# A hierarchical mixture-of-experts block: float32 rows kept once, a later residual, two more weight slots

## The chip, the cores and the metric

The kernel runs on one core of a Trainium2 chip. The metric is the device time of one launch in microseconds (us). The engines that matter are TensorE (PE in the rows, its weight loads PEld), VectorE (DVE), ScalarE (ACT), GpSimd (POOL) and SyncE (SP), whose queue issues the large loads from HBM. All data is float32 in HBM; all weights are read once.

## The reference

One layer over 256 latent tokens of width 1024. A mixing half (retention over tokens and a 256-token context, a convolution branch, gates, an output projection) gives `mix`; then

```python
h_lat = _layernorm(ALPHA * h_lat + gt_m * mix, p['ln1_g'], p['ln1_b'])
moe = _hier_moe(_modulate(h_lat, sh_f, sc_f), p)
h_lat = _layernorm(ALPHA * h_lat + gt_f * moe, p['ln2_g'], p['ln2_b'])
```

`_hier_moe` picks for each token the best of four groups and the two best of its eight experts, and adds up, weighted, what the 32 experts give:

```python
for e in range(N_EXPERTS):
    h = jax.nn.silu(t @ p['w_exp_gate'][e]) * (t @ p['w_exp_up'][e])
    y = y + combine[:, e:e + 1] * (h @ p['w_exp_down'][e])
```

An expert has a gate and an up matrix of 1024 x 512 and a down matrix of 512 x 1024, 2 MiB each.

## The kernel before

The mixing half fills PE until about 511 us. Its result plus ALPHA times the input is `xr`, two tiles of 128 tokens by 1024. Then comes the **head of the experts**, once: the statistics of the first layer norm and the router's scores; two calls of `rank` on DVE (groups, then experts in the group), which give the mask `M`; three small matmuls on PE (`ppos`) that turn the mask into each token's place among an expert's tokens; and `gather(0)`.

The normalized rows are kept without the layer norm's gain and bias (these and the modulation are in the columns `fsc` and `fsh`). They are kept as a pair: `xr` is normalized in place (one tile on ACT, one on POOL), `xns[0]` is its value rounded to fp32r, a shorter float format, and `xns[1]` is what the rounding left out, also in fp32r; POOL forms half of that (`xn_low(G, ...)`), DVE the rest in two pieces. The sum of both products gives a float32 row to enough places. After gather 0 is set up, DVE overwrites `xr` with ALPHA times the layer norm's full result, the residual `yacc`; for this PE has spread the gain and bias `ln1` over all partitions (`lnb`, eight K=1 matmuls of a high and low part).

`gather(c)` serves experts 4c to 4c+3. DVE writes a one-hot matrix (`ohr`, later `ohq`) of 256 places; for each of eight slices k of the width, PE multiplies the rows with it (line 1351: two token tiles times two parts, four matmuls of 128 x 128 by 256), and ACT or DVE moves the result out with scale and bias into `xe[c]`. It is a generator that yields after every two k, so four pieces of it are spread over a pair of experts.

The experts run in 16 pairs, e0 = 0, 2, ..., 30, in `expert_pair`: gate and up of the one (`hidden`, line 1365: 64 places as stationary columns, in two halves side by side), of the other, transposes, and the down products (line 1465). What the down products give is put back to tokens one pair later by `scatter` (line 1406), into four PSUM banks that collect over all pairs; `flush` adds them to `yacc` in the last pair. Every second pair (e0 = 2, 6, ..., 26) carries the gather of the next four experts. After pair e0 = 28 a branch on a count of tokens leads to `overflow()`, which this data doesn't need. The second layer norm's gain and bias (`ln2`) are loaded after pair e0 = 16 and spread by PE after pair e0 = 20 (line 1635), each of four banks copied out by ACT.

The **weights** come in tiles of 1 MiB, twelve to a pair (eight of gate and up, four of down), in the order of use (`plan`). `load_to(n)` puts loads up to the nth on SP's queue, in order; the tags of the list `slots` say which SBUF buffer each takes. A load waits until the last reader of its buffer's former tenant is done, and all behind it on the queue wait too. `first` has 19 entries; after that each turn has 16, from the 100th tile on 15, as other tiles need buffers. Tiles 0 to 18 are asked for before the experts begin (`NL`), the rest at the start and the end of every pair.

Of the kernel before, what the change touches and what calls it, by code (L numbers as in the profile page):

```python
# [8 lines left out]
F32 = mybir.dt.float32  # L9
# [10 lines left out]
P = 128  # L20
# [14 lines left out]
NL = 9, 5, 0, 6, 6, 5, 7, 8, 19, 6  # L35
NCYC = 100
# [3 lines left out]
LN2 = 16, 20  # L40
# [5 lines left out]
def tile_block(ctx, tc, a, out):  # L46
# [30 lines left out]
    def gload(dst, src):  # L77
        nc.gpsimd.dma_start(dst, src)
# [871 lines left out]
    def rows_load2(_):  # L950
        for q in range(2):
            ln1[q] = row1(f"ln1_{q}")
            G.memset(ln1[q], 0.0)
            for i, nm in enumerate(("ln1_g", "ln1_b")):
                gload(ln1[q][64 * i:64 * i + 33:32], a[nm].rearrange("o (c q f) -> q (o c) f", c=2, q=2)[q])
# [20 lines left out]
    ln1 = {}  # L976
# [294 lines left out]
    xn_low(V, 1, 1)  # L1271
# [14 lines left out]
    lnb = {}  # L1286
    for cb in range(2):
        for i in range(2):
            lnb[i, cb] = bank("y", f"lnb{i}{cb}")
            p0 = 64 * i + 32 * cb  # L1290
            for q in range(2):
                T.matmul(lnb[i, cb], oner[p0:p0 + 1], lns[q][p0:p0 + 1], start=(q == 0), stop=(q == 1))
# [3 lines left out]
    ppos = bank("gu", "ppos", (P, 2, 32))  # L1296
# [40 lines left out]
    def gather(c):  # L1337
        ohr = ohrs[c] = ohq[:, c % 2] if c else sb.tile([P, 2, 4, CAP], F32R, tag="rope", name="ohr", bufs=1)
# [3 lines left out]
        xe[c] = big("X8" if c == 1 else "U8", [P, 8, 4 * CAP], f"xe{c}")  # L1342
# [3 lines left out]
        for k2 in (2, 3, 0, 1):  # L1346
            ps = bank("mi", f"ga{c}_{k2}", (P, 2, 4 * CAP))
            for kk in range(2):
                k = 2 * k2 + kk
                for i, (t, s) in enumerate(((0, 0), (0, 1), (1, 0), (1, 1))):  # L1350
                    T.matmul(ps[:, kk], xns[s][:, t, k // 4, k % 4], ohr[:, t], start=(i == 0), stop=(i == 3))  # L1351
            for kk in range(2):
                k = 2 * k2 + kk
                if kk and c:
# [62 lines left out]
    def expert_pair(e0, side):  # L1417
# [5 lines left out]
        else:  # L1423
            hs = [hidden(e0)]
            if last:
                for cb in range(2):
                    scatter(e0 - 2, cb)
                flush()
# [97 lines left out]
    def overflow():  # L1526
# [12 lines left out]
        for k in range(8):  # L1539
            for s in range(2):  # L1540
                pt = bank("mi", f"oxt{k}_{s}", (P, 2, P))
                for t in range(2):
                    T.transpose(pt[:, t], xns[s][:, t, k // 4, k % 4].bitcast(F32), ident)
                if s == 0:
                    V.tensor_copy(xoT[:, k], pt)
                else:
                    V.tensor_add(xoT[:, k], xoT[:, k], pt)
            V.tensor_scalar(xoT[:, k], xoT[:, k], fsc[:, k:k + 1], fsh[:, k:k + 1], op0=ALU.mult, op1=ALU.add)
# [40 lines left out]
    xn_low(V, 1, 0)  # L1589

    yacc = xr
    for cb in range(2):
        cs = slice(512 * cb, 512 * cb + 512)
        for i, op in enumerate((ALU.mult, ALU.add)):
            for t in range(2):
                if i:
                    V.scalar_tensor_tensor(yacc[:, t, cs], lnb[1, cb], ALPHA, yacc[:, t, cs], op0=ALU.mult, op1=op)
                else:
                    V.scalar_tensor_tensor(yacc[:, t, cs], xr[:, t, cs], ALPHA, lnb[0, cb], op0=ALU.mult, op1=op)
# [3 lines left out]
    def rest():  # L1603
# [3 lines left out]
        V.tensor_copy(ohq[:, 0], ohrs[0].bitcast(F32))  # L1607
# [6 lines left out]
    ln2 = None  # L1614
    for e0 in range(0, NE, 2):
# [11 lines left out]
        if e0 == LN2[0]:  # L1627
            ln2 = big("Y8", [P, 2, D], "ln2")
            gload(ln2[0:1, 0], a["ln2_g"])
            gload(ln2[0:1, 1], a["ln2_b"])  # L1630
        if e0 == LN2[1]:
# [64 lines left out]
```

## Time and profile before

| | us |
|---|---|
| three runs | 996.44, 996.86, 998.81 |
| median | 996.86 |
| the profiled execution, its own time | 1000.41 |
| its span in the trace | 998.6 |
| PE busy in the span | 942.7 (94%) |
| DVE busy | 506.3 (51%) |
| ACT busy | 310.2 (31%) |
| POOL busy | 104.4 (10%) |
| mean granted TensorE clock | 0.977 |

PE is the busy engine of the span as a whole. The span has three stretches with different limits: the mixing half up to 511 us, the head of the experts up to 529 us, where little runs beside the chain through DVE, and the experts, in whose second half the DMA engines move 420 GB/s without a break. Which of two limits holds in the experts is read from the waits at single weight tiles and from the lengths of pairs, since a share of busy time averages over all of this.

### The profile page before, as it was taken

Reading aid. Unit: us, or ns where it says so; the run is one execution under the profiler, and the core shown is the slowest. Engines: PE = TensorE matmul, PEld = TensorE weight load, DVE = VectorE, ACT = ScalarE, POOL = GpSimd, SP = SyncE. Lnnn points to the kernel's source line nnn. Section 1 sums busy time; section 2 is a strip of 40 time slices with the busy share of each in tenths; the row PEclk is TensorE's granted clock in tenths of the full one; section 3 lists DMA queues with packets and bytes.
Section 4 is the critical chain, followed back from the end, with each engine's and each line's share of the span. In section 5 each row is a group of like instructions: output and inputs, shape, how many; then the busy total and the mean of one; then the engine's idle time right before and its main releaser. Section 6 shows DMA issues by size and latency. Waiting matters only on the chain. (4 is left out here: it accounts for less than half of the span.)

```text
span 998.6 us, 15317 instructions
## 1 busy us (share of the span) xinstructions
PE 942.7 (94%) x6354; PEld 691.5 (69%) x6354; DVE 506.3 (51%) x976; ACT 310.2 (31%) x458; POOL 104.4 (10%) x122
## 2 busy tenths in 40 slices
PE   3999999999999999989989999999999989999884
PEld 2799879779879869889976655656565554655452
DVE  1377988897886996785884111222221111222135
ACT  3357735443543444375443111111110101111010
POOL 1002120210210020721520000000000000000001
PEclk9699999999999999999999999999999998999998
DMA  8795634544374347759986899999999999999991
GB/s 269 231 362 202 220 107 129 214 143 160 115 253 142 136 139 239 268 185 289 348 331 272 346 419 419 421 420 420 420 419 420 421 419 421 421 420 420 421 366 44
DMA packets 92424, 294.81 MB, mean 295 GB/s; under 512 B 6921, under 2 KB 37825, under 8 KB 68288
## 3 DMA queue, kind: packets, MB, share of 16 engines
q1 hardware_dynamic: 91360, 293.31, 76.4%
q0 software_dynamic: 992, 0.49, 0.4%
q8 instruction: 51, 0.84, 0.4%
q14 instruction: 21, 0.17, 0.1%
HBM read 292.71 MB, written 1.06 MB: 294 GB/s over the span
## 5 line engine op out<-in xcount | busy, mean ns | idle before, releaser
L1465 PE MATMUL dn<-wdown,hT 128*64 128x512 f32 (+1 forms) x528 | 120.7, 584 | 6.3 <-DMA wdown<-in_w_exp_down_dram 6.0
L1365 PE MATMUL gu<-wgate,xe 128*64 128x256 f32 x1024 | 122.5, 391 | 2.2 <-DVEq L1625 2.2
L1365 PE MATMUL gu<-wup,xe 128*64 128x256 f32 x1024 | 118.3, 380 | 4.2 <-DMA wup<-in_w_exp_up_dram 4.1
L1371 DVE TENSOR_TENSOR h<-h,gu 128x256 f32<-128x256 f32 x32 | 13.5, 421 | 198.2 <-ACT h L1370 198.2
L404 DVE SCALAR_TENSOR_TENSOR slab<-zp,taps,slab 128x256 f32<-128x256 f32 x232 | 107.1, 515 | 0.0
L1365 PEld LDWEIGHTS gu<-wgate,xe 128*64 128x64 f32 x1024 | 74.5, 141 | 45.8 <-issue 10.3
L1365 PEld LDWEIGHTS gu<-wup,xe 128*64 128x64 f32 x1024 | 74.1, 137 | 42.8 <-DMA wup<-in_w_exp_up_dram 8.2
L1465 PEld LDWEIGHTS dn<-wdown,hT 128*64 128x64 f32 x528 | 37.6, 136 | 76.6 <-issue 59.9
L1370 ACT ACTIVATE h<-gu 128x256 f32<-128x256 f32 x32 | 12.3, 385 | 210.9 <-PE gu L1365 210.8
L1480 DVE SCALAR_TENSOR_TENSOR dl<-dn,ws,ohq 128x512 fp32r<-128x512 f32 x30 | 22.5, 751 | 104.3 <-ACT ohq L1479 104.3
L1479 ACT ACTIVATE ohq<-dn,ws 128x512 fp32r<-128x512 f32 x30 | 20.6, 688 | 125.4 <-PE dn L1465 122.7
L98 PE MATMUL ya<-rT,qro 128*128 128x256 f32 x128 | 36.7, 286 | 2.6 <-DVE rT L750 2.6
L97 PE MATMUL glu<-ulh,qz 128*128 128x256 f32 x128 | 37.5, 293 | 0.0
L99 PE MATMUL ya<-rT,qro 128*128 128x256 f32 x128 | 36.6, 286 | 0.8 <-DVE qro L164 0.8
L97 PE MATMUL ya<-rT,qro 128*128 128x256 f32 x128 | 36.9, 288 | 0.0
L99 PE MATMUL gt<-ulh,qg 128*128 128x256 f32 x128 | 35.8, 280 | 1.1 <-DVE qg L164 1.1
L98 PE MATMUL glu<-ull,qz 128*128 128x256 f32 x128 | 36.8, 287 | 0.0
L99 PE MATMUL glu<-ulh,qz 128*128 128x256 f32 x128 | 36.7, 287 | 0.0
L97 PE MATMUL gt<-ulh,qg 128*128 128x256 f32 x128 | 36.6, 286 | 0.0
L1358 ACT ACTIVATE xe<-ga,cf 128x256 f32<-128x256 f32 x36 | 19.8, 564 | 52.5 <-PE ga L1351 52.5
L98 PE MATMUL gt<-ull,qg 128*128 128x256 f32 x128 | 35.8, 279 | 0.0
L1351 PE MATMUL ga<-ohq,xnh 128*128 128x256 f32 x112 | 30.4, 306 | 0.0
(477 smaller groups left out, 2159.1 us busy)
## 6 DMA issues: line engine op xcount, KB each, us to landing
wgate<-in_w_exp_gate_dram SPq DMA_DIRECT2D x64, 1024.0 KB, 19.8
wup<-in_w_exp_up_dram SPq DMA_DIRECT2D x64, 1024.0 KB
wdown<-in_w_exp_down_dram SPq DMA_DIRECT2D x60, 1024.0 KB, 19.8
wa<-in_w_ada_dram SPq DMA_DIRECT2D x24, 1024.0 KB, 9.4
wz<-in_w_in_dram SPq DMA_DIRECT2D x16, 512.0 KB, 7.5
wro<-in_w_ret_out_dram SPq DMA_DIRECT2D x8, 1024.0 KB
wg<-in_w_in_dram SPq DMA_DIRECT2D x8, 1024.0 KB, 9.9
wk<-in_w_in_dram SPq DMA_DIRECT2D x4, 1024.0 KB, 12.3
```

The costliest lines, as they stand in the source:

```text
L97: T.matmul(ps, st[0], mv[0], start=start, stop=False)
L98: T.matmul(ps, st[0], mv[1], start=False, stop=False)
L99: T.matmul(ps, st[1], mv[0], start=False, stop=stop)
L404: V.scalar_tensor_tensor(dst, zp[:, ct, j:j + NT], taps[:, ct, j:j + 1], ac[ct], op0=ALU.mult, op1=ALU.add)
L1351: T.matmul(ps[:, kk], xns[s][:, t, k // 4, k % 4], ohr[:, t], start=(i == 0), stop=(i == 3))
L1358: S.activation(xe[c][:, k], ps[:, kk], AF.Identity, scale=fsc[:, k:k + 1], bias=fsh[:, k:k + 1])
L1365: T.matmul(ps[64 * hf:64 * hf + 64, j], xe[c][:, k, CAP * i:CAP * i + CAP], w[:, k % 4, NT * hf:NT * hf + NT], start=start, stop=stop)
L1370: S.activation(h, ps[:, 0], AF.Silu)
L1371: V.tensor_mul(h, h, ps[:, 1])
L1465: T.matmul(ps[64 * x:64 * x + 64], hT[x][:, ch % 2, 64 * (ch // 2):64 * (ch // 2) + 64], w, start=(ch == 0), stop=(ch == 3))
L1479: S.activation(dh, ps, AF.Copy, scale=ws)
L1480: V.scalar_tensor_tensor(dl, ps, ws, dh.bitcast(F32), op0=ALU.mult, op1=ALU.subtract)
```

## The change

Three things are changed.

- **The rows are kept once.** `xn` is one float32 tile pair, written by four ACT operations straight from the unnormalized `xr`. The split, POOL's and DVE's subtractions, and the split and the eight broadcasts of `ln1` are gone. `gather` multiplies `xn` and the one-hot as full float32: two matmuls for each k instead of four. The two matmuls that put zeros into the first experts' banks are written ahead of `ppos`; in gather 0 the odd slices are now moved out by DVE, as in the other gathers.
- **The residual is formed in the middle of the experts.** `ln1` is loaded after pair e0 = 14 into a tile `lnv`; after pair e0 = 18 PE spreads it with four K=1 matmuls (`l1r`), and DVE forms the new tile `yacc` from these and `xn` with eight operations. `ln2` is loaded into the same `lnv` after pair e0 = 20 and spread after pair e0 = 24.
- **Two more slots.** `first` has 21 entries, the turns after it 19, from the 96th tile on 17, the last 24 tiles 12. One weight tile (the ninth) is asked for two steps earlier in the output projection. `flush` and the scatter of pair e0 = 28 are written between gate and up of expert 30, no longer between the experts 30 and 31.

The core of the diff:

```diff
-NL = 9, 5, 0, 6, 6, 5, 7, 8, 19, 6
-NCYC = 100
+NL = 9, 5, 0, 6, 6, 5, 7, 9, 21, 6
+NCYC = 96
-LN2 = 16, 20
+LNS = 14, 20, 18, 24
...
-    body = ["X8"] + ["W8"] * 3 + ["Q8", "W8"] + ["Q8"] * 2 + ["X8"] * 2
-    first = ["S8", "X8"] + ["Y8"] * 4 + ["zp", "U8"] + body + ["Y8"]
-    cyc = ["S8", "X8"] + ["Y8"] * 3 + body[1:] + ["Y8"]
-    slots = first + ["S8", "X8"] + ["Y8"] * 4 + ["U8"] + body[1:] + ["Y8"]
+    body = ["W8"] * 3 + ["Q8", "W8"] + ["Q8"] * 2 + ["X8"] * 2
+    first = ["S8", "X8"] + ["Y8"] * 4 + ["zp"] + ["U8"] * 2 + ["X8"] + body + ["Y8"] * 2
+    full = ["S8", "X8"] + ["Y8"] * 4 + ["U8"] * 2 + body + ["Y8"] * 2
+    cyc = ["S8", "X8"] + ["Y8"] * 3 + ["U8"] * 2 + body + ["Y8"]
+    slots = first + full
     while len(slots) < NCYC:
-        slots += ["S8", "X8"] + ["Y8"] * 4 + body[1:] + ["Y8"]
+        slots += full
...
-            if cb == 1 and kq == 0:
+            if cb == 0 and kq == 2:
                 step(lambda _: load_to(NL[7]))
...
-    xns = [big("U8", [P, 2, D], f"xn{s}", F32R).rearrange("p t (r k q) -> p t r k q", r=2, k=4) for s in "hl"]
-
-    def xn_low(E, t, r):
-        E.tensor_sub(xns[1][:, t, r], xrk[:, t, r], xns[0][:, t, r].bitcast(F32))
+    xn = big("U8", [P, 2, D], "xn").rearrange("p t (r k q) -> p t r k q", r=2, k=4)
...
-    S.activation(xr[:, 0], xr[:, 0], AF.Identity, scale=rs1[:, 0:1], bias=nb1[:, 0:1])
-    G.tensor_scalar(xr[:, 1], xr[:, 1], rs1[:, 1:2], nb1[:, 1:2], op0=ALU.mult, op1=ALU.add)
-    for t in range(2):
-        S.activation(xns[0][:, t], xrk[:, t], AF.Copy)
-    xn_low(G, 0, slice(0, 2))
+    for r in (1, 0):
+        for t in range(2):
+            S.activation(xn[:, t, r], xrk[:, t, r], AF.Identity, scale=rs1[:, t:t + 1], bias=nb1[:, t:t + 1])
...
-                for i, (t, s) in enumerate(((0, 0), (0, 1), (1, 0), (1, 1))):
-                    T.matmul(ps[:, kk], xns[s][:, t, k // 4, k % 4], ohr[:, t], start=(i == 0), stop=(i == 3))
+                for t in range(2):
+                    T.matmul(ps[:, kk], xn[:, t, k // 4, k % 4], ohr[:, t].bitcast(F32), start=(t == 0), stop=(t == 1))
...
+        if e0 == LNS[2]:
+
+            yacc = big("Y8", [P, 2, D], "yacc")
+            for cb in range(2):
+                cs = slice(512 * cb, 512 * cb + 512)
+                yk = yacc[:, :, cs].rearrange("p t (q k) -> p t k q", k=4)
+                for i in range(2):
+                    ps = bank("mi", f"l1r{cb}{i}")
+                    T.matmul(ps, onef[0:1], lnv[0:1, i, cs], start=True, stop=True)
+                    pk = ps.rearrange("p (q k) -> p k q", k=4)
+                    for t in range(2):
+                        if i == 0:
+                            V.scalar_tensor_tensor(yk[:, t], pk, ALPHA, xn[:, t, cb], op0=ALU.mult, op1=ALU.mult)
+                        else:
+                            V.scalar_tensor_tensor(yacc[:, t, cs], ps, ALPHA, yacc[:, t, cs],
+                                                   op0=ALU.mult, op1=ALU.add)
```

How the instructions stand at two places, in the order of each engine's queue (a number behind a tile's name only tells buffers apart). PE in the head, from the broadcasts to the first gather, before:

```order
L1292 MATMUL lnb_4896<-lns_4786,oner 128x512
L1283 MATMUL clkq_4899<-oner,ident 128x128 x6
L1297 LDWEIGHTS tri
L1297 MATMUL ppos<-M,tri 128x32
L1298 LDWEIGHTS oneh
L1298 MATMUL ppos<-M,oneh 128x32
L1299 LDWEIGHTS tri
L1299 MATMUL ppos<-M,tri 128x32
L1283 MATMUL clkq_4910<-oner,ident 128x128 x5
L1351 MATMUL ga_2_4935<-ohr,xnh 128x256
L1351 MATMUL ga_2_4935<-ohr,xnl 128x256
```

and after:

```order
L1272 MATMUL gu_4874<-oner,zero 128x512
L1272 MATMUL gu_4875<-oner,zero 128x512
L1267 MATMUL clkq_4878<-oner,ident 128x128 x6
L1277 LDWEIGHTS tri
L1277 MATMUL ppos<-M,tri 128x32
L1278 LDWEIGHTS oneh
L1278 MATMUL ppos<-M,oneh 128x32
L1279 LDWEIGHTS tri
L1279 MATMUL ppos<-M,tri 128x32
L1267 MATMUL clkq_4889<-oner,ident 128x128 x5
L1331 MATMUL ga_2_4905<-ohr,xn 128x256 x4
L1331 MATMUL ga_3_4912<-ohr,xn 128x256 x4
```

Eight broadcasts are gone, the two zero matmuls (`gu`) stand ahead of `ppos`, and a bank of the gather (`ga`, two k) has four matmuls from one `xn` instead of eight from `xnh` and `xnl`.

DVE in the same place, from the second rank's first product to the end of the head, before:

```order
L1253 TENSOR_TENSOR rkec<-rkec,before 128x128
L1254 TENSOR_TENSOR rkec<-rkec 128x128
L1255 TENSOR_REDUCE rke<-rkec 128x16
L1269 TENSOR_SCALAR m_4858<-rke 128x16
L1263 TENSOR_TENSOR M<-m_4858,og 128x64
L1215 TENSOR_TENSOR xnl<-xr,xnh 128x512
L1340 TENSOR_TENSOR ohr<-ppos,slot 128x256 x2
L1344 COPY pos<-ppos 128x64
L1215 TENSOR_TENSOR xnl<-xr,xnh 128x512
L1599 SCALAR_TENSOR_TENSOR xr<-xr,lnb_4887 128x512 x2
L1597 SCALAR_TENSOR_TENSOR xr<-lnb_4890,xr 128x512 x2
```

and after:

```order
L1238 TENSOR_TENSOR rkec<-rkec,before 128x128
L1239 TENSOR_TENSOR rkec<-rkec 128x128
L1240 TENSOR_REDUCE rke<-rkec 128x16
L1254 TENSOR_SCALAR m_4846<-rke 128x16
L1248 TENSOR_TENSOR M<-m_4846,og 128x64
L1320 TENSOR_TENSOR ohr<-ppos,slot 128x256 x2
L1324 COPY pos<-ppos 128x64
L1335 TENSOR_SCALAR xe_4903<-ga_2_4905,cf 128x256
L1335 TENSOR_SCALAR xe_4903<-ga_3_4912,cf 128x256
```

The two subtractions (`xnl`) and the residual (`xr`, `lnb`) have left this place; the gather's own copies follow the one-hot `ohr`.

PE between pair e0 = 18 and the next, after (before, the gate follows the last matmul of the gather):

```order
L1443 MATMUL dn_1_6541<-wdown_1_6386,hT_6510 64x512
L1331 MATMUL ga_1_6553<-ohq,xn 128x256 x4
L1605 MATMUL l1r_6577<-lnv,oner 128x512
L1605 MATMUL l1r_6581<-lnv,oner 128x512
L1605 MATMUL l1r_6585<-lnv,oner 128x512
L1605 MATMUL l1r_6589<-lnv,oner 128x512
L1345 MATMUL gu_6601<-wgate_0_6388,xe_6408 64x256 x8
```

The four broadcasts `l1r` stand between the last piece of the gather and the gate of expert 20.

## Rows read from the trace of the kernel before

**Rows 1.** Windows of the core: length, busy us by engine, clock, DMA share, GB/s.
```profile
600.50:653.00 52.50, 52.50 (x389) 31.92 (x388) 10.71 (x24) 6.55 (x12) 0.00 (x0) 1.00 1.01 420
758.20:949.20 191.00, 179.83 (x1205) 101.31 (x1204) 33.62 (x76) 22.73 (x41) 1.08 (x2) 0.98 1.01 420
```

**Rows 2.** Timeline of PE, pairs e0 = 16 and 20: start, us, instruction, idle before.
```profile
758.20 1.08 PE L1465 MATMUL dn<-wdown,hT 128*64 128x512 f32 x4
...
823.12 5.36 PE L1465 MATMUL dn<-wdown,hT 128*64 128x512 f32 x22 [1.41 <-DMA wdown<-in_w_exp_down_dram]
828.41 1.12 PE L1635 MATMUL l2r<-ln,oner 1*128 1x512 f32 x2
...
833.79 6.29 PE L1365 MATMUL gu<-wgate,xe 128*64 128x256 f32 x32
839.92 3.62 PE L1365 MATMUL gu<-wup,xe 128*64 128x256 f32 x32
```

**Rows 3.** Timeline of PE, end of pair e0 = 28, gate of expert 30.
```profile
943.79 5.36 PE L1465 MATMUL dn<-wdown,hT 128*64 128x512 f32 x22 [1.42 <-DMA wdown<-in_w_exp_down_dram]
951.33 5.36 PE L1365 MATMUL gu<-wgate,xe 128*64 128x256 f32 x32 [2.17 <-DVEq L1625]
```

**Rows 4.** PE's waits from 540 us on: total, times, longest.
```profile
PE dn L1465 <- DMA wdown<-in_w_exp_down_dram: 6.0, 6, 1.4
PE gu L1365 <- DMA wup<-in_w_exp_up_dram: 4.1, 7, 1.2
```

**Rows 5.** Windows as in group 1: gather 0, behind the broadcasts, expert 30's gate.
```profile
832.30:839.10 6.80, 6.80 (x28) 3.05 (x29) 0.00 (x0) 1.13 (x2) 0.00 (x0) 0.50 1.01 417
951.80:955.20 3.40, 3.40 (x19) 2.41 (x17) 0.00 (x0) 0.00 (x0) 0.00 (x0) 0.50 1.02 419
524.65:528.20 3.55, 3.55 (x18) 3.47 (x17) 3.55 (x7) 1.02 (x2) 0.00 (x0) 0.50 0.01 2
```

**Rows 6.** Timeline of SP's queue, the last issue ahead of the experts.
```profile
511.64 19.75 SPq L75 DMA_DIRECT2D wup<-in_w_exp_up_dram  x2
```

**Rows 7.** Timeline of PE, one piece of gather 1 and the gate behind it.
```profile
561.93 0.38 PE L1351 MATMUL ga<-ohq,xnh 128*128 128x256 f32 x1
...
562.26 0.28 PE L1351 MATMUL ga<-ohq,xnh 128*128 128x256 f32 x1
...
562.83 0.28 PE L1351 MATMUL ga<-ohq,xnl 128*128 128x256 f32 x1
563.04 3.24 PE L1365 MATMUL gu<-wgate,xe 128*64 128x256 f32 x28
```

**Rows 8.** Timeline of PE, a retention product in full float32.
```profile
169.03 7.07 PE L686 MATMUL o<-v,dp 128*128 128x256 f32 x32
```

**Rows 9.** Timeline of DVE in the head of the experts.
```profile
518.02 0.28 DVE L1252 TENSOR_TENSOR rkec<-ig 128x128 f32<-128x128 f32 x1
518.22 2.95 DVE L1253 TENSOR_TENSOR rkec<-rkec,before 128x128 f32<-128x128 f32 x1
...
522.30 1.07 DVE L1215 TENSOR_TENSOR xnl<-xr,xnh 128x512 fp32r<-128x512 f32 x1
...
526.24 1.30 DVE L1597 SCALAR_TENSOR_TENSOR xr<-lnb,xr 128x512 f32<-128x512 f32 x2
```

**Rows 10.** Timeline of POOL in the head.
```profile
518.09 2.93 POOL L1215 TENSOR_TENSOR xnl<-xr,xnh 128x1024 fp32r<-128x1024 f32 x1 [2.06 <-ACT xnh L1241]
```

**Rows 11.** Timeline of PE in the head: ppos, gather 0, zeros, first gate.
```profile
522.44 0.18 PE L1297 MATMUL ppos<-M,tri 128*128 128x32 bf16 x1 [4.03 <-DVE M L1263]
...
524.65 0.56 PE L1351 MATMUL ga<-ohr,xnh 128*128 128x256 f32 x1
...
528.34 0.80 PE L1385 MATMUL gu<-xnh,zero 1*128 1x512 f32 x2
529.07 1.30 PE L1365 MATMUL gu<-wgate,xe 128*64 128x256 f32 x10
```

**Rows 12.** Timeline of ACT in the head.
```profile
515.96 3.99 ACT L1241 ACTIVATE xnh<-xr 128x1024 fp32r<-128x1024 f32 x2
```

More of the change, by code (lines that the diff above doesn't have):

```diff
@@ L950, in rows_load2 @@
     def rows_load2(_):
[L951 to L955, printed above, removed]
         cols(cf[:, 0], arow_flat(8))
@@ L975, in tile_block @@
     tmp = big("Y8", [P, 2, D], "tmp")
-    ln1 = {}
     def weave(main, *sides):
@@ L1283, in keep_clock2 @@
                 T.matmul(pclk[:, 0:P], ident, onef, start=True, stop=True)
[L1286 to L1292, printed above, removed]
+    gu0 = [bank("gu", f"gu{e}", (P, 2, NT)) for e in range(2)]
+    for e in range(2):
+        T.matmul(gu0[e], zero, oner[0:1, None, :].to_broadcast([1, 4, P]), start=True, stop=False)
     keep_clock2(KC4)
-    ppos = bank("gu", "ppos", (P, 2, 32))
+    ppos = bank("mi", "ppos", (P, 2, 32))
     T.matmul(ppos[:, 0], tri, M[:, 0], start=True, stop=True)
@@ L1337, in gather @@
     def gather(c):
-        ohr = ohrs[c] = ohq[:, c % 2] if c else sb.tile([P, 2, 4, CAP], F32R, tag="rope", name="ohr", bufs=1)
+        ohr = ohrs[c] = ohq[:, c % 2] if c else sb.tile([P, 2, 4, CAP], F32, tag="rope", name="ohr", bufs=1)
         for t in range(2):
@@ L1372, in swiglu, with hidden @@
         return h
-    def hidden(e):
+    def hidden(e, between=None):
         ps = bank("gu", f"gu{e}", (P, 2, NT))
         for j in range(2):
+            if j and between:
+                between()
             for k in range(8):
@@ L1381, in first_hidden @@
     def first_hidden():
-        ps = [bank("gu", f"gu{e}", (P, 2, NT)) for e in range(2)]
-        for e in range(2):
-            T.matmul(ps[e], zero, xns[0][0:1, 0, 0], start=True, stop=False)
+        ps = gu0
         for r in (1, 0):
@@ L1423, in expert_pair @@
         else:
[L1424 to L1428, printed above, removed]
+            hs = [hidden(e0, flush if last else None)]
             next(side, None)
@@ L1539, in overflow @@
         for k in range(8):
[L1540 to L1548, printed above, removed]
+            pt = bank("mi", f"oxt{k}", (P, 2, P))
+            for t in range(2):
+                T.transpose(pt[:, t], xn[:, t, k // 4, k % 4], ident)
+            V.tensor_scalar(xoT[:, k], pt.rearrange("p t n -> p (t n)"), fsc[:, k:k + 1], fsh[:, k:k + 1],
+                            op0=ALU.mult, op1=ALU.add)
         with tc.For_i(0, NE, 1) as e:
@@ L1588, in tile_block @@
     next(g0)
[L1589 to L1599, printed above, removed]
     next(g0)
@@ L1606, in rest @@
         weights()
[L1607 removed]
+        V.tensor_copy(ohq[:, 0], ohrs[0])
         pcnt = bank("mi", "pcnt")
@@ L1612, in rest @@
         V.tensor_copy(cnt_i, cnt)
-    ln2 = None
+    lnv = yacc = None
     for e0 in range(0, NE, 2):
@@ L1626, in tile_block @@
                 overflow()
[L1627 to L1631, printed above, removed]
+        if e0 in LNS[0:2]:
+            n = LNS.index(e0) + 1
+            if n == 1:
+                lnv = big("Y8", [P, 2, D], "lnv")
+            gload(lnv[0:1, 0], a[f"ln{n}_g"])
+            gload(lnv[0:1, 1], a[f"ln{n}_b"])
+        if e0 == LNS[2]:
+            yacc = big("Y8", [P, 2, D], "yacc")
+            for cb in range(2):
+                cs = slice(512 * cb, 512 * cb + 512)
[4 more added lines that the diff above has]
+                    pk = ps.rearrange("p (q k) -> p k q", k=4)
+                    for t in range(2):
+                        if i == 0:
+                            V.scalar_tensor_tensor(yk[:, t], pk, ALPHA, xn[:, t, cb], op0=ALU.mult, op1=ALU.mult)
+                        else:
+                            V.scalar_tensor_tensor(yacc[:, t, cs], ps, ALPHA, yacc[:, t, cs],
+                                                   op0=ALU.mult, op1=ALU.add)
+        if e0 == LNS[3]:
             for i in range(4):
@@ L1634, in tile_block @@
                 cs = slice(512 * (i % 2), 512 * (i % 2) + 512)
-                T.matmul(ps, onef[0:1], ln2[0:1, i // 2, cs], start=True, stop=True)
-                S.activation(ln2[:, i // 2, cs], ps, AF.Copy)
+                T.matmul(ps, onef[0:1], lnv[0:1, i // 2, cs], start=True, stop=True)
+                S.activation(lnv[:, i // 2, cs], ps, AF.Copy)
     mv2 = small((2, 2), "mv2")
@@ L1651, in tile_block @@
         if t:
-            E.tensor_mul(o, o, ln2[:, 0, cs])
-            E.tensor_add(o, o, ln2[:, 1, cs])
-        else:
-            E.scalar_tensor_tensor(o, o, mv2[:, 0, 0:1], ln2[:, 0, cs], op0=ALU.subtract, op1=ALU.mult)
-            E.scalar_tensor_tensor(o, o, rs2[:, 0:1], ln2[:, 1, cs], op0=ALU.mult, op1=ALU.add)
+            E.tensor_mul(o, o, lnv[:, 0, cs])
+            E.tensor_add(o, o, lnv[:, 1, cs])
+        else:
+            E.scalar_tensor_tensor(o, o, mv2[:, 0, 0:1], lnv[:, 0, cs], op0=ALU.subtract, op1=ALU.mult)
+            E.scalar_tensor_tensor(o, o, rs2[:, 0:1], lnv[:, 1, cs], op0=ALU.mult, op1=ALU.add)
         nc.sync.dma_start(out[0, P * t:P * t + P, cs], o)
```

11 lines of the change are left out of this document (3 added, 8 removed).

## Prediction, made before the changed kernel was run

> **What bounds the kernel now.** I read the timeline of TensorE (PE) from the router to the last expert first. Expert pair number n (e0 = 2n) starts its down projection at 600.5 us for n = 2 and 653.0 for n = 4, and in the 52.50 us between PE is never idle while the DMA engines are busy at a share of 1.01 [rows 1]. So two pairs cost PE 52.5 us, 26.25 each. Their 24 weight tiles cost the DMA more: PE is twice let go inside a down projection by the weight that lands last, at 823.12 and at 943.79 [rows 2, 3], four pairs or 48 tiles apart, so a tile takes 120.67 / 48 = 2.514 us and two pairs 60.3 us. PE starts with a stock of prefetched tiles, eats it at 3.9 us a pair, and waits from pair 8 on: the list of PE's waits names the down weights (6.0 us) and the up weights (4.1 us) [rows 4].
>
> These two lists show only time in which PE stood plainly idle; the whole wait I take from lengths. From the down projection of pair 8 (758.20 [rows 2]) to the end of pair 14's (949.15: the gate that starts at 951.33 had 2.17 us of idle before it [rows 3]) are 190.95 us. Six pairs need 157.5 and the last down projection 7.1 (32 matmul records of 0.22 us, as 22 of them in 5.36 show [rows 2]). The four broadcasts of the second layer norm take 828.41 to 833.79 = 5.4, and the gate behind them took 6.29 instead of 3.62 [rows 2], at a granted clock of 0.50 [rows 5], 2.7 more. That sums to 172.7, so **18.3 us are waits for weights**. The stage from the first gate (529.07) to 949.15 is thus set by the DMA at its end, and PE would need 420.1 - 18.3 = 401.8 us for it. What follows 949.15 is the same in both kernels but for details.
>
> **The change, part by part.** *Two more slots.* They bring every tile forward by up to 2 x 2.514 = 5.0 us. Today the queue stands still after its nineteenth tile: one SP row of two issues spans 511.64 to 531.39, the second waiting until the first gate has been read [rows 6], and the DMA share falls to 0.01 [rows 5]. If gather 0 ends sooner, this stop ends sooner too. Together 5 to 9 us, of which up to 2 may be lost in the next stop; the DMA would let pair 14 end near 943. That is worth something only while the DMA sets the end.
>
> *The gather in plain float32.* Before, one k of a gather is four fp32r matmuls (high and low part, two token tiles). Their starts are (562.83 - 562.26) / 5 = 0.114 us apart [rows 7], so 0.46 for a k. After, it is two matmuls of the same 128x256 shape on full float32. Such matmuls exist in the retention: 32 records, which are 16 instructions in the code, start at 169.03 and last 7.07, the last record itself 0.38 of it, so a start comes every 6.69 / 31 = 0.216 us and an instruction takes two records, 0.43 [rows 8]. A k then costs 0.86, 0.40 more, and a gather of eight k 3.2 more. Seven gathers stand inside the pairs: +22.6; the second half of gather 0 adds 1.6. Nothing hides this, since PE has no idle time in pairs 1 to 7, and later its idle time is what the waits leave. **+24.2.** The lower bound: a piece of two k lasts 1.11 us today (561.93 to 563.04), of which 0.92 is the eight starts; if the slower matmuls swallowed the 0.2 at the borders, 28 pieces would give back 5.6. I keep the border, because it is PE's own.
>
> In the Trainium skill, "FP8 and Floating Point Precision", section "TensorE Precision Notes", true FP32 takes four passes through the array and the reduced form reads the value once. By that rule a k would be 2 x 4 passes against 4 x 1, 0.92 us against 0.46, and the sum 3.5 us higher; the trace's 0.43 against 0.114 is a ratio of 3.8, and I go by the trace.
>
> *The head.* With the low part POOL's subtraction goes. It ran from 518.09 for 2.93 us, and in exactly that time VectorE's (DVE's) rank comparison of 518.22 took 2.95, where the multiplication of the same shape before it took 0.28 [rows 9, 10]. That delay lies on the path: the mask is built from it, PE stood idle 4.03 us until ppos at 522.44 [rows 11]. -2.67. The subtraction of 1.07 us that DVE did between mask and one-hot [rows 9] goes too, but the one-hot must wait for ppos anyway: -0.5. The new xn comes from four ScalarE activations instead of one on ScalarE and one on POOL and then two conversions, which took 3.99 [rows 12]; at 1.0 us each they end near 519, before the one-hot. So gather 0 starts near 524.65 - 3.2 = 521.45. Its sixteen records would take 3.46 at 0.216; today's sixteen took 3.69 at a clock of 0.50 [rows 5, 11]. The two zero matmuls (528.34 to 529.07, 0.73) are done ahead in the idle time. First gate near 524.95: **-4.1**. The bounds: if the clock falls again, the sixteen take 6.9 and the gain is 0.6; the four LN broadcasts and DVE's four residual pairs (1.30 us a row of two [rows 9]) lie beside other work and go for nothing.
>
> *The residual formed after pair 9.* Four K=1 broadcasts come on PE's queue, behind the last gather piece of that pair and ahead of pair 10's gate. Nothing like it with DVE behind it is in the trace; the nearest is the second layer norm's block, 5.4 us with ScalarE copying each bank [rows 2]. Two banks turn around, so the third and fourth matmul wait for DVE to finish with the first and second, two operations of 0.65 each [rows 9] or about double if the strided reads are slow: 3.6 to 8 us. I take **+5.4**. Queued behind it on PE is the whole of pair 10, and on DVE the next product; no stock of weights helps that. A fall of the clock as after the second layer norm's block would add 2.7.
>
> *Moved at no cost.* The second layer norm's broadcasts come two pairs later, same price. The loads of ln1 on POOL's queue come two pairs (52.5 us) ahead of their use. On SP one weight tile goes ahead of a mixing weight; at most one tile, 2.5 us, and the queue ahead of it has no stop. The flush is written into the last pair behind the end of the waits. After the overflow branch the gate of expert 30 ran 5.36 instead of 3.62 [rows 3, 5]; 0 to 1.7 could return.
>
> **The sum.** Without waits PE would end pair 14 at 949.15 - 4.1 + 24.2 + 5.4 - 18.3 = 956.4, some 13 us after the DMA's 943. The waits are gone, and what they were is now work. The stock also lasts in between: at pair 8, where PE runs dry today, PE would be 4 x 3.2 + 1.6 - 4.1 = 10.3 us later and the tiles about 6 earlier, and from there the stock shrinks by only (60.3 - 55.7) / 2 = 2.3 a pair. So **+7.2 us**: the profiled execution's 1000.41 (span 998.6) would become 1007.6. It lies 3.55 above the median of 996.86; I carry the difference over: **1004.1**.
>
> **Rivals.**
> (a) *The border is swallowed and the clock holds*: -5.6 for the borders or -2.7 -1.7 for no fall after the broadcasts and the branch. That is +1.6 to +2.8: 998.5 to 999.7. For it: no row of today has a full-array float32 matmul behind 64-column ones. Against: the second block of broadcasts is the same as today, and today the clock falls there.
> (b) *The float32 matmul costs no more than two fp32r.* The gate's records, also float32, come 0.113 apart (3.62 / 32 [rows 2]); if a gather record did so, a k would stay at 0.45, PE would end pair 14 near 932 and the DMA would set the end, 5.0 + 4.1 us earlier: about 987.8. It decides where a gather costs less than 1.4 us more than today (13.4 us of lead over 7.5 gathers). Against it: the gate's are 64-column tiles of the array, the retention's are the gather's full shape.
> (c) *The clock falls in the head and after the new broadcasts*: +3.5 and +2.7 on top, 1007.6 to 1010.3. For it: PE will still sit idle for about 1 us ahead of ppos, and today the clock was at half from there to 528 [rows 5].
> (d) *The change works as a prefetch*: the DMA remains the bound all through and PE has slack for the gather. Then -7 or so; that needs PE idle of more than 30 us where I find 18.3. It goes with (b).
>
> **How the numbers follow.** Forecast with its own bounds (1000.5 to 1007.5): 0.58. (a) 0.14, (b) and (d) 0.11, (c) 0.17. The range leaves out (b) and the outermost of (c): 998 to 1011. A measurement of this kernel can tell about 0.3%, 3 us, from no change: faster 0.11, within 0.14, slower 0.75.
>
> **What would show it.** In the gather line of the changed kernel the records are 0.216 apart and a piece lasts 1.9 us; two pairs take 55.7 us instead of 52.5; the waits of PE for down and up weights are all but gone, and the DMA share of 758 to 949 is below 1, with SP waiting for PE. The rank comparison takes 0.3 us and the first gate starts near 525. After pair 9 stands a stretch of about 5 us of l1r. I am wrong if the weights still let PE go late in pairs 9 to 14, if a gather record comes every 0.11 us, or if the first gate stays near 529.

## The result, and the profile after

The changed kernel takes 1006.25 us (median of four, 1006.12 to 1007.59) where the kernel before takes 997.84 (four, 996.44 to 998.86): a ratio of 1.0088, with an interval of 1.0070 to 1.0106. It is slower by 8.4 us; the forecast was 7.2 slower, 1004.1 in a range of 998 to 1011. In a second set of runs it was 1.0075 (1.0051 to 1.0098). The profiled execution took 1007.59 with a span of 1005.7, 7.1 more than the 998.6 before.

PE's waits from 520 us on, in the changed kernel (total, times, longest; to be read against [rows 4]):

```profile
PE gu L1345 <- DMA wdown<-in_w_exp_down_dram: 2.2, 1, 2.2
PE ht L1417 <- DVE hT L1419: 1.7, 2, 0.9
PE l1r L1605 <- DVE yacc L1609: 0.8, 1, 0.8
PE l2r L1617 <- ACT lnv L1618: 0.7, 1, 0.7
PE l1r L1605 <- DVE xe L1335: 0.2, 1, 0.2
```

The down and up weights are gone from the list. The one row that still names a weight is the 2.2 us at the overflow branch, the same gap as before, put down to another releaser. PE now sets the end of every pair, as the window of two pairs and that of the last 201.1 us ahead of the end of pair 14 show (columns as in [rows 1]):

```profile
600.53:656.21 55.68, 55.68 (x390) 33.81 (x389) 10.70 (x24) 6.55 (x12) 0.00 (x0) 1.00 1.01 420
757.20:958.30 201.10, 199.38 (x1299) 115.61 (x1294) 41.35 (x88) 23.48 (x43) 0.97 (x2) 0.97 1.00 412
```

Two pairs take 55.68 us instead of 52.50, and PE is busy for 199.4 of the 201.1 us; before, it was busy for 180 of the 191 us from the down projection of pair 8 on. In turn SP's queue now waits for PE to free buffers. Its waits for PE of more than 1 us, from 740 us to the end of pair 14, after and then before:

```profile
SPq L75 <- PE dn L1443: 33.7, 10, 8.3
SPq L75 <- PE gu L1345: 28.3, 17, 10.3
```

```profile
SPq L75 <- PE gu L1365: 1.1, 4, 0.3
```

The head, PE and then DVE (start, duration, instruction; to be read against [rows 11] and [rows 9]):

```profile
519.68 0.18 PE L1277 MATMUL ppos<-M,tri 128*128 128x32 bf16 x1 [0.97 <-DVE M L1248]
...
520.98 3.69 PE L1331 MATMUL ga<-ohr,xn 128*128 128x256 f32 x16
524.60 1.96 PE L1345 MATMUL gu<-wgate,xe 128*64 128x256 f32 x16
```

```profile
512.64 0.33 DVE L1216 BATCH_NORM_AGGREGATE mv<-st 128x2 f32<-128x12 f32 x2
...
517.93 0.28 DVE L1237 TENSOR_TENSOR rkec<-ig 128x128 f32<-128x128 f32 x1
518.13 0.28 DVE L1238 TENSOR_TENSOR rkec<-rkec,before 128x128 f32<-128x128 f32 x1
```

The rank multiplication takes 0.28 us instead of 2.95, PE's idle time ahead of `ppos` is 0.97 instead of 4.03, gather 0 runs at a granted clock of 1.00 (window 520.98 to 524.60), and the first gate starts at 524.60 instead of 529.07. Counted from the same row of the first layer norm, which was

```profile
512.32 0.32 DVE L1229 BATCH_NORM_AGGREGATE mv<-st 128x2 f32<-128x12 f32 x2
```

in the kernel before, the first gate comes after 11.96 us instead of 16.75.

A piece of a gather and the block behind pair e0 = 18, PE and DVE:

```profile
804.25 1.99 PE L1331 MATMUL ga<-ohq,xn 128*128 128x256 f32 x8
806.17 1.12 PE L1605 MATMUL l1r<-lnv,oner 1*128 1x512 f32 x2
807.48 1.12 PE L1605 MATMUL l1r<-lnv,oner 1*128 1x512 f32 x2 [0.18 <-DVE xe L1335]
809.44 3.46 PE L1605 MATMUL l1r<-lnv,oner 1*128 1x512 f32 x4 [0.84 <-DVE yacc L1609]
812.84 5.49 PE L1345 MATMUL gu<-wgate,xe 128*64 128x256 f32 x32
```

```profile
807.34 1.96 DVE L1609 SCALAR_TENSOR_TENSOR yacc<-l1r,xn 128x512 f32<-128x512 f32 x2
809.15 1.26 DVE L1611 SCALAR_TENSOR_TENSOR yacc<-l1r,yacc 128x512 f32<-128x512 f32 x2
811.24 1.97 DVE L1609 SCALAR_TENSOR_TENSOR yacc<-l1r,xn 128x512 f32<-128x512 f32 x2 [0.83 <-PE l1r L1605]
```

The piece lasts 1.92 us (804.25 to 806.17), against 1.11 [rows 7]. The block lasts 6.67 us (806.17 to 812.84): its first bank is read by DVE's strided pair, 0.98 us an operation, the other form takes 0.63. The gate behind it takes 5.49 instead of 3.62. The second half of the block and the gate stand at a low granted clock, 0.54 and 0.65 in the mean (the column behind the five engines):

```profile
809.44:812.84 3.40, 3.40 (x4) 0.88 (x5) 2.57 (x4) 0.00 (x0) 0.48 (x1) 0.54 1.01 419
812.84:818.16 5.32, 5.32 (x33) 3.17 (x34) 1.48 (x3) 0.00 (x0) 0.49 (x1) 0.65 1.01 413
```

At the end of the stage:

```profile
951.22 7.09 PE L1443 MATMUL dn<-wdown,hT 128*64 128x512 f32 x32
960.51 3.67 PE L1345 MATMUL gu<-wgate,xe 128*64 128x256 f32 x32 [2.21 <-DMA wdown<-in_w_exp_down_dram]
```

Pair 14 (e0 = 28) ends at 960.51 - 2.21 = 958.3, 9.15 us later than 949.15; the last down projection runs 7.09 us without a stop where it was stopped twice.

For all that follows one length is useful: **from the start of the first gate to the end of pair 14**, since what lies ahead of it differs by some us from one execution to the next (in a second trace of the changed kernel the first gate starts at 520.90). It is 420.1 us before and 433.7 after. The times of one kernel on one chip differ by up to 0.8%, in step with the mean granted clock (the kernel before: 994.29 us at 0.981, 1002.48 at 0.973), which is as much as the whole change.

### The profile page after: what moved, and what is told of

Read it like the earlier page. It is cut to its first block, busy times and chain, and to the rows that moved or that the text cites. A ratio compares the mean times of both kernels' runs of the same rounds, so it can differ in the third digit from the quotient of the medians.

```text
span 1005.7 us, 15338 instructions
## 1 busy us (share of the span) xinstructions
PE 962.8 (96%) x6354; PEld 704.2 (70%) x6354; DVE 504.4 (50%) x978; ACT 307.1 (31%) x453; POOL 98.2 (10%) x114
## 4 chain that ended last, share of the span: by engine, by line
PE 84%; issue 4%; DMA 4%; DVE 4%; POOL 2%; ACT 2%; SPq 0%; POOLq 0%; ACTq 0%
PE gu L1345 23%; PE dn L1443 11%; PE ga L1331 6%; PE y L1386 3%; DMA wa<-in_w_ada_dram 2%; PE o L686 2%; PE glu L97 2%; PE glu L99 2%; PE glu L98 2%; PE kp L97 2%; PE kp L99 1%; PE kp L98 1%; PE sc L667 1%; PE ya L98 1%; PE ya L97 1%
## 5 line engine op out<-in xcount | busy, mean ns | idle before, releaser
L1443 PE MATMUL dn<-wdown,hT 128*64 128x512 f32 (+1 forms) x528 | 114.7, 583 | 0.0
L1331 PE MATMUL ga<-ohq,xn 128*128 128x256 f32 x224 | 55.8, 392 | 0.0
L1331 PEld LDWEIGHTS ga<-ohq,xn 128*128 128x128 f32 x224 | 40.2, 189 | 15.7 <-issue 11.1
L1335 DVE TENSOR_SCALAR xe<-ga,cf 128x256 f32<-128x256 f32 x32 | 17.4, 544 | 56.2 <-ACT xe L1338 52.8
L97 PE MATMUL glu<-ulh,qz 128*128 128x256 f32 x128 | 37.3, 291 | 0.0
## 6 DMA issues: line engine op xcount, KB each, us to landing
wg<-in_w_in_dram SPq DMA_DIRECT2D x8, 1024.0 KB, 10.1
```

The source lines that it names most:

```text
L97: T.matmul(ps, st[0], mv[0], start=start, stop=False)
L1331: T.matmul(ps[:, kk], xn[:, t, k // 4, k % 4], ohr[:, t].bitcast(F32), start=(t == 0), stop=(t == 1))
L1443: T.matmul(ps[64 * x:64 * x + 64], hT[x][:, ch % 2, 64 * (ch // 2):64 * (ch // 2) + 64], w, start=(ch == 0), stop=(ch == 3))
```

## The experiments

Each run was made beside runs of the kernel before on its own chip; the ratio is to those.

**The gather at its old price.** Edit to the changed kernel:

```diff
-                for t in range(2):
-                    T.matmul(ps[:, kk], xn[:, t, k // 4, k % 4], ohr[:, t].bitcast(F32), start=(t == 0), stop=(t == 1))
+                for i, t in enumerate((0, 0, 1, 1)):
+                    T.matmul(ps[:, kk], xn[:, t, k // 4, k % 4], ohr[:, t], start=(i == 0), stop=(i == 3))
```

(with `xn` and `ohr` of type F32R; it leaves out the low part and counts each rounded row twice).

> The changed kernel with its gather at the old price: per slice k four fp32r matmuls again (all four on the one tile, which is rounded to fp32r, so the low part is left out and the rows count twice; the work is that of the kernel before). Slots, head and late residual stay. Theory (the float32 gather is what PE pays, and without it the DMA sets the end of pair 14 again, near 943 instead of 958.3): about 15 us less than the changed kernel, 990 to 993, with PE waiting for weights again in the pairs before 943. Rival 1 (the loss lies in the new residual block and the clock, the gather is hidden in the old waits): 1001 or more. Rival 2 (two more slots bring nothing to the DMA side): end of pair 14 near 949, 997.

Measured: 987.84 us (984.26 to 991.74) against 998.95, ratio 0.9882 (0.9843 to 0.9921), some 2 us below what was expected. First gate and the gate behind pair 14:

```profile
521.74 2.00 PE L1345 MATMUL gu<-wgate,xe 128*64 128x256 f32 x16
...
939.28 3.67 PE L1345 MATMUL gu<-wgate,xe 128*64 128x256 f32 x32 [2.17 <-DVEq L1588]
```

Pair 14 ends at 937.1, a length of 415.4 us: 18.3 less than the changed kernel's, for one change, the form of the gather's matmuls. PE waits at the weights again (`dn <- DMA wdown` 1.6 us in the waits, the same kind of row as [rows 4]). The gather is what the change pays.

**The gather alone.** Edit to the kernel before:

```diff
-                for i, (t, s) in enumerate(((0, 0), (0, 1), (1, 0), (1, 1))):
-                    T.matmul(ps[:, kk], xns[s][:, t, k // 4, k % 4], ohr[:, t], start=(i == 0), stop=(i == 3))
+                for t in range(2):
+                    T.matmul(ps[:, kk], xns[0][:, t, k // 4, k % 4].bitcast(F32), ohr[:, t].bitcast(F32),
+                             start=(t == 0), stop=(t == 1))
```

> The kernel before with nothing changed but the gather: two full float32 matmuls per k of the rounded high tile (the low part is still formed but not used). Theory: first gate 3.3 us later (sixteen records at a clock of 0.50), then PE needs 420.1 - 18.8 + 23.9 = 425.2 us to the end of pair 14: 957.6, waits for weights nearly gone, 1006 (1004 to 1008); then the other edits of the change come to about nothing in sum. Rival (the waits of 18 us swallow the gather): the DMA still sets the end, 3 us later at most, 998 to 1001.

Measured: 1006.02 us (1003.49 to 1007.21) against 998.95, ratio 1.0059 (1.0041 to 1.0077). In PE's timeline:

```profile
523.64 5.11 PE L1351 MATMUL ga<-ohr,xnh 128*128 128x256 f32 x16
528.67 0.73 PE L1386 MATMUL gu<-xnh,zero 1*128 1x512 f32 x2
529.33 1.95 PE L1366 MATMUL gu<-wgate,xe 128*64 128x256 f32 x16
...
836.77 5.04 PE L1636 MATMUL l2r<-ln,oner 1*128 1x512 f32 x6 [0.69 <-ACT ln L1637]
841.73 6.50 PE L1366 MATMUL gu<-wgate,xe 128*64 128x256 f32 x32
...
958.36 3.67 PE L1366 MATMUL gu<-wgate,xe 128*64 128x256 f32 x32 [2.22 <-DVEq L1626]
```

The length is 956.14 - 529.33 = 426.8 us, 6.7 more than before, and no wait for a weight is left. So the gather alone makes the kernel nearly as slow as the whole change does, and the rest of the change comes to little in sum. The 18 us of waits swallowed three quarters of the 24, not all. One detail was off: the clock stayed low for part of the sixteen records only (5.11 us, not 6.9; the granted clock of 523.64 to 528.67 is 0.70). The length was expected at 425.2; the 1.6 us above it are the block of the second layer norm and the gate behind it, which take 6.77 (834.96 to 841.73) and 6.50 us here and 5.38 and 6.29 in the kernel before [rows 2].

**Without the block of the residual.** Edit to the changed kernel, which leaves gain and bias out of the residual: the four broadcasts and eight operations become, for each half of the width,

```diff
+                for t in range(2):
+                    V.tensor_scalar(yk[:, t], xn[:, t, cb], ALPHA, None, op0=ALU.mult)
```

> The changed kernel without the broadcasts of ln1 in the middle: the residual is ALPHA times xn by four DVE operations (gain and bias of the first layer norm are left out of it), PE has nothing to do there. Theory (PE sets the end, so the 6.7 us of the block and the 1.9 us of the half clock behind it go through in full): 8.5 us less, 997 to 999. Rival 1 (only the four matmuls count, 1.7 us; the rest is hidden): 1004.5. Rival 2 (the weights set the end after pair 9): 1006.

Measured: 996.74 us (993.55 to 998.29) against 998.95, ratio 0.9971 (0.9953 to 0.9990). First gate at 522.55, pair 14 ends at 947.84: a length of 425.3, 8.4 less than the changed kernel's 433.7, as 6.67 + 1.87 asks. The block goes through to the end in full.

**Two slots fewer**, run on two chips, the second time beside the changed kernel itself. Edit:

```diff
-NL = 9, 5, 0, 6, 6, 5, 7, 9, 21, 6
+NL = 9, 5, 0, 6, 6, 5, 7, 9, 19, 6
...
-    first = ["S8", "X8"] + ["Y8"] * 4 + ["zp"] + ["U8"] * 2 + ["X8"] + body + ["Y8"] * 2
-    full = ["S8", "X8"] + ["Y8"] * 4 + ["U8"] * 2 + body + ["Y8"] * 2
-    cyc = ["S8", "X8"] + ["Y8"] * 3 + ["U8"] * 2 + body + ["Y8"]
+    first = ["S8", "X8"] + ["Y8"] * 4 + ["zp"] + ["U8"] + ["X8"] + body + ["Y8"]
+    full = ["S8", "X8"] + ["Y8"] * 4 + ["U8"] + body + ["Y8"]
+    cyc = ["S8", "X8"] + ["Y8"] * 3 + ["U8"] + body
```

> The changed kernel with two slots fewer: 19 first, then 17 a turn, then 15. Theory (PE sets the end with some 13 us of lead over the DMA, so the slots bring nothing): the same as the changed kernel within 1 us, 1005 to 1007.5, with no waits for weights. Rival (the slots still pay for themselves): 5 us more, 1011.

> The changed kernel with two slots fewer, beside the changed kernel on the same chip. Theory (PE sets the end, the slots bring nothing): the same within 1.5 us. Rival 1 (the slots pay for themselves): 5 us slower. Rival 2 (the slots cost something, as the first comparison by ratios hints): 3 to 4 us faster.

> The changed kernel as it is, beside the same with two slots fewer, on one chip. Theory: 1.0088 of the kernel before, as measured first.

Measured: first 1004.56 us, ratio 1.0048 (1.0031 to 1.0064), which hinted at a gain; then 1006.03 (1004.24 to 1009.10) beside 1005.39 (1003.61 to 1009.50) for the changed kernel, both 1.0075 of the kernel before. The lengths are 432.3, 432.3 and, with the slots, 433.4 (433.7 in the first trace). In the changed kernel the two slots bring nothing, and the hint of a loss by them did not come back in the times. The lengths are 1.1 to 1.4 us shorter without the slots, and this lies in the two blocks of broadcasts and the gates behind them. Of the residual's block, third and fourth broadcast and the gate behind (first run), then the window of the two broadcasts:

```profile
808.26 2.14 PE L1605 MATMUL l1r<-lnv,oner 1*128 1x512 f32 x4 [0.84 <-DVE yacc L1609]
810.34 5.36 PE L1345 MATMUL gu<-wgate,xe 128*64 128x256 f32 x32
```

```profile
808.26:810.34 2.08, 2.08 (x5) 0.56 (x5) 1.92 (x4) 0.00 (x0) 0.48 (x1) 1.00 1.02 425
```

The block lasts 5.35 us here (804.99 to 810.34) and 5.48 in the second run, against 6.67 and 6.95 in the two traces with the slots. DVE's strided operations take 0.98 in all four; what differs is the granted clock in the second half, 1.00 and 0.93 against 0.54 and 0.50. Whether the slots have a part in that is not shown.

**The same slots where the DMA sets the end.** First a gather that costs PE little: two fp32r matmuls for each k, with the rows rounded to fp32r once and no low part (types as in the run with four).

```diff
-                    T.matmul(ps[:, kk], xn[:, t, k // 4, k % 4], ohr[:, t].bitcast(F32), start=(t == 0), stop=(t == 1))
+                    T.matmul(ps[:, kk], xn[:, t, k // 4, k % 4], ohr[:, t], start=(t == 0), stop=(t == 1))
```

> The changed kernel with xn and the one-hot rounded to fp32r and two fp32r matmuls per k: half of the matmuls of the kernel before, a quarter of the passes; the rows are rounded once. Theory (with the gather cheap the DMA sets the end of pair 14, and the run with four fp32r matmuls showed 937): PE gets 17 us more slack that it can't use, only the first gate comes 0.9 us earlier: 984 to 988. Rival (PE still set the end in that run): 970 to 975.

> The kernel with two fp32r matmuls per k and two slots fewer (19 first, 17 and 15 a turn). Theory (here the DMA sets the end of pair 14, and each slot brings all tiles forward by one transfer of 2.51 us): from the first gate to the end of pair 14 it is 5.0 us longer than with 21 slots, 420.0 instead of 415.0 us, the length of the kernel before; 992 in all. Rival (the slots bring less, since the next stop of the queue is longer): 1 to 3 us.

Measured: 987.17 us (982.85 to 988.65) against 998.92, ratio 0.9888 (0.9865 to 0.9911); with two slots fewer 991.86 (989.02 to 994.74) against 998.39, ratio 0.9936 (0.9911 to 0.9962). First gate and the gate behind pair 14, with 21 slots and then with 19:

```profile
518.60 2.10 PE L1345 MATMUL gu<-wgate,xe 128*64 128x256 f32 x16 [0.31 <-ACT xe L1338]
...
935.65 3.67 PE L1345 MATMUL gu<-wgate,xe 128*64 128x256 f32 x32 [2.17 <-DVEq L1588]
```

```profile
519.68 2.10 PE L1345 MATMUL gu<-wgate,xe 128*64 128x256 f32 x16 [0.32 <-ACT xe L1338]
...
941.90 3.67 PE L1345 MATMUL gu<-wgate,xe 128*64 128x256 f32 x32 [2.19 <-DVEq L1588]
```

The lengths are 414.9 and 420.0 us. The second is that of the kernel before, which had 19 slots too; the first is that of the run with four fp32r matmuls (415.4), though the gather keeps PE busy for 21.9 us there instead of 36.0. So with a cheap gather the DMA sets this length and nothing else, and two slots are worth 5.1 us of it, two transfers of 2.51.

**The broadcasts one by one.** Edit to the changed kernel: the four of `ln1` and the four of `ln2` are written as generators, and one is taken ahead of each half of the gate and up steps of pairs e0 = 20 and 24:

```diff
...
-        expert_pair(e0, side)
+        thin = iter(())
+        if e0 == LNS[2] + 2:
+            yacc = big("Y8", [P, 2, D], "yacc")
+            thin = l1_spread()
+        if e0 == LNS[3]:
+            thin = l2_spread()
+        expert_pair(e0, side, thin)
```

> The changed kernel with its float32 gather, but each of the eight broadcasts (four of ln1, four of ln2) put on its own between parts of pairs e0 = 20 and 24 instead of two blocks. Theory (PE sets the end; in the two blocks it waits for banks and runs at half clock behind them): the blocks took 6.7 + 5.2 us and the half clock 1.9 + 2.8, eight matmuls alone cost 3.4, so 13 us less than the changed kernel: 992 to 995, clock 1.00 through the whole stretch. Rival (the waits of the blocks move into the pairs, since DVE has the same work): 3 to 5 us less, 1001 to 1003.

> Both: two fp32r matmuls per k, and the eight broadcasts spread. Theory (the DMA sets the end of pair 14, so PE's 13 us are eaten by waits for weights): within 2 us of the kernel with two fp32r matmuls and the broadcasts in blocks. Rival (PE sets the end): 10 to 13 us less than that.

Measured, with the float32 gather: 999.24 us (996.71 to 1000.05) against 998.92, ratio 0.9999 (0.9982 to 1.0017), between the two expectations. Timeline of PE in pair e0 = 20:

```profile
805.24 1.12 PE L1588 MATMUL l1r<-lnv,oner 1*128 1x512 f32 x2
806.29 3.67 PE L1345 MATMUL gu<-wgate,xe 128*64 128x256 f32 x32
809.90 1.12 PE L1588 MATMUL l1r<-lnv,oner 1*128 1x512 f32 x2
810.95 3.67 PE L1345 MATMUL gu<-wup,xe 128*64 128x256 f32 x32
```

The gates behind take 3.67, the granted clock of both stretches of broadcasts is 1.00, and PE waits for no bank. But a broadcast takes 1.05 us (805.24 to 806.29), not the 0.43 for which it was reckoned: 0.43 is the price of 256 columns [rows 8], and these have 512. Eight cost 8.4, not 3.4, so 16.6 - 8.4 = 8.2 could be saved, and the length went from 433.7 to 426.4, by 7.3. With the cheap gather the spread brought 984.08 us (982.81 to 988.64), ratio 0.9861 (0.9825 to 0.9896), a length of 415.0 as without it: PE's time turned into waits (down weights 6.2 us, up weights 4.1):

```profile
PE dn L1446 <- DMA wdown<-in_w_exp_down_dram: 6.2, 7, 1.4
PE gu L1345 <- DMA wup<-in_w_exp_up_dram: 4.1, 9, 0.5
```

**POOL's work put back.** Edit to the changed kernel, behind the four activations:

```diff
+    tm5 = tmp.rearrange("p t (r k q) -> p t r k q", r=2, k=4)
+    G.tensor_sub(tm5[:, :, 1], xrk[:, :, 1], xn[:, :, 1])
```

> The changed kernel with one subtraction on POOL put back beside the rank in the head (128 x 1024, its result used by nobody). Theory (DVE's rank multiplication stands still while POOL subtracts): it takes 2.9 us instead of 0.28, ppos and the first gate come 2.7 us later, and as PE sets the end all of it arrives at the end: 1009; if PE's longer idle time drops the clock again, gather 0 takes 6.9 us instead of 3.6 and it is 1012. Rival (the stall of the kernel before had another cause): 1006, multiplication at 0.3.

Measured: 1009.95 us (1007.73 to 1013.31) against 998.92, ratio 1.0122 (1.0094 to 1.0150), beside 1.0088 for the changed kernel, 3.4 us, though the two intervals overlap. POOL and DVE in the head:

```profile
513.80 2.87 POOL L1229 TENSOR_TENSOR tmp<-xr,xn 128x1024 f32<-128x1024 f32 x1 [22.09 <-ACT xn L1227]
```

```profile
508.85 0.32 DVE L1216 BATCH_NORM_AGGREGATE mv<-st 128x2 f32<-128x12 f32 x2
...
513.93 2.89 DVE L1238 TENSOR_TENSOR rkec<-ig 128x128 f32<-128x128 f32 x1
516.74 0.28 DVE L1239 TENSOR_TENSOR rkec<-ig 128x128 f32<-128x128 f32 x1
516.95 0.28 DVE L1240 TENSOR_TENSOR rkec<-rkec,before 128x128 f32<-128x128 f32 x1
```

POOL starts 0.4 us earlier in the chain here than in the kernel before (0.13 us ahead of the rank's first comparison, where it was 0.28 behind it), and so another DVE operation is met, that comparison, which takes 2.89 us where it takes 0.29 else; the multiplication, which was expected to be the one, takes 0.28. PE's idle time ahead of `ppos` grows to 3.57 us, and gather 0 takes 4.1 us instead of 3.6: the clock falls for a part of it (0.86 in 520.82 to 524.95). From the layer norm's row to the first gate (524.95) it is 16.10 us instead of 11.96, so the subtraction costs the head 4.1 us in this trace. The stall is POOL's doing, whichever operation of DVE meets it. "SBUF — State Buffer" of the Trainium skill, section "SBUF: two separate sides", calls the port pair that DVE and GpSimd share an exclusive lock, held for a whole instruction. The trace agrees: POOL's subtraction ends at 516.67 and DVE's comparison, which started behind it, at 516.82.

## Why the prediction was right, point by point

**What bounds.** Right. The waits of [rows 4] are gone, PE is busy through the second half, SP waits for PE, and the forms with a cheap gather show the other bound. One sign did not show: the DMA share was to fall below 1 and is 1.00, at 412 GB/s instead of 420. That bound was set a little too late: the DMA's end was put near 943, and by the 415 us it would be 524.6 + 415.0 = 939.6. The two slots came in full and nothing was lost in the next stop, of which the text had allowed 2 us.

**The gather, +24.2.** Right. Two pairs were to take 55.7 us and take 55.68, 3.18 more than [rows 1]; a piece takes the 1.92 that 0.216 a record and the border give. Behind the first gate the gather's rows sum to 59.62 us where they were 35.77, 23.9 more. The lower bound, in which the border is swallowed, falls, and with it the first form of rival (a): the piece of 1.92 carries the border still. Of its second form, no fall of the clock, the part at the branch came true (below), the part behind the broadcasts did not: the gates there take 5.49 and 6.46. Rival (b), a float32 record at the price of the gate's 64-column one, falls by the same row, and (d) with it. By the four passes of true FP32 in the Trainium skill, which were weighed there ("FP8 and Floating Point Precision", section "TensorE Precision Notes"), a gather would have cost 0.5 us more than that, as an estimate; the trace stays with 0.86 for a k.

**The head, -4.1.** Right: 4.47 by the clock of the two traces, 529.07 to 524.60, and 4.8 from the layer norm's row on. The stall on DVE went, and the clock held, so that part of rival (c) fell. (The text has two names exchanged: the operation of 518.22 that stalled is the rank's multiplication, the one ahead of it a comparison.) That POOL caused the stall was argued from two rows that stand side by side; putting the work back has now shown it.

**The residual, +5.4.** The path was right, the sum left a term out. The block takes 6.67 us and the gate behind it 1.87 more than at full clock, 8.5 in all, and without the block the length is 8.4 us shorter. In the first run with two slots fewer the clock held through the block, and it took 5.35, the forecast's size, although the strided operations take 0.98 and not 0.65. So some 3.2 us of the 8.5 are the fallen clock, 1.3 in the second half of the block and 1.9 behind it. The text priced such a fall at 2.7, gave it to rival (c) and left it out of the sum: this is the term that was mis-sized, by 3.1. Most of the block is not waiting either: PE waits 1.02 us by its rows, and each broadcast keeps it busy for 1.05 even at full clock, a price that the text didn't have.

**The waits, -18.3.** Going back from the result: 420.1 - W + 23.9 for the gather's own part behind the first gate + 8.5 for the block is 433.7 where W is 18.8. The gather alone gives the same: 420.1 - 18.8 + 23.8 and the 1.6 of its second layer norm are 426.7, where 426.8 was measured. The count by lengths held within half a microsecond; the two rows of the wait list, 10.1 us, would have been too few by 8.

**The sum.** Pair 14 ends 9.15 us later, where 7.2 was said: -4.5 + 23.9 + 8.5 - 18.8. Behind it 2 us come back, most of them at the gate of expert 30, which takes 3.67 us where it took 5.36 [rows 3]. The text had named this as 0 to 1.7 and left it out. That the change brings it is not shown: all other traces have 3.67 there, that of the gather alone with its old tail too, and also that of the cheap gather with single broadcasts, in which PE stops in the last down projection as before; why the clock fell there in the one trace of the kernel before stays open. So it is luck that the span's 7.1 hits the forecast's 7.2: the block was too cheap by 3.1 and the tail too dear by 2, with smaller errors of the tail's sign in head, gather and waits. The medians differ by 8.4, with 1.8 us of interval either way.

**Slips in the working.** They change neither the sum nor a chance. Rival (b) decides below 1.4 us a gather, as it says, but by (24.2 - 13.4) / 7.5 and not by the 13.4 / 7.5 in its bracket. The range does not leave out the outermost of (c): that ends at 1010.3, inside 1011. The rows of [rows 5] belong, from the first to the third, to the gate behind the broadcasts, expert 30's gate and gather 0.

**Which version is best.** Head, slots and residual of the change with two fp32r matmuls per k and the broadcasts one by one: 984.08 us, 0.9861 of the kernel before, 22 us below the changed kernel. It differs in what it computes by the rounding of the rows to fp32r, in the experts' input and in the residual. The same with the broadcasts in blocks is 0.9888, and the intervals of the two overlap.

## What to carry to other kernels

A prefetch slot is worth one transfer only where the transfers set the end, and a cheaper or dearer matmul counts only where the matmuls do: count each stage's length on both sides before pricing an edit, and take the waits from lengths of whole units, since a list of waits shows fewer. An engine's idle time at the end of a stage is a store that pays for new work just once; here 18 us of it paid for three quarters of 24. Before saving a buffer by a wider number format, look for the price of that format in the trace, in the same shape of tile.

## What had not been expected

- A broadcast of one row over all partitions (K=1, 512 columns, float32) keeps PE busy for 1.05 us, more than twice a full-array float32 matmul of 256 columns (0.43). In the block of the changed kernel PE waits 1.02 us in all and is busy for the rest.
- A block of four such broadcasts leaves the granted clock low behind it: in all eleven traces with such a block the gate behind it takes 5.2 to 6.6 us instead of 3.6. Of the same eight, taken one at a time between gates, none does with the float32 gather (3.67); with the cheap gather one of the eight gates takes 5.36, behind waits of 0.79 and 0.97 us. Whether the waits or the row of K=1 matmuls lower the clock is not shown.
- DVE reading PSUM and writing a float32 tile, both with a stride of four elements, takes 0.98 us for 128 x 512; without it 0.63.
